# Three modulations' first column groups move from TensorE to VectorE, GLA's last gates move behind its results, and one set of norm factors goes

## The chip, the cores and the metric

The kernel runs as one program on one core of a Trainium2 chip. The metric is the device time of one execution in microseconds (us); the time of the kernel before is the median of three runs. All arithmetic is fp32. The engines are TensorE (PE, matmuls), VectorE (DVE), ScalarE (ACT), GpSimd (POOL) and SyncE (SP), whose queue issues nearly all DMAs.

## The reference

Two blocks of two layers each work on 256 tokens x and 256 context tokens, both of width 1024. Each layer has a modulation, a mixer (an attention with a hyena branch in the first block, DeltaNet and GLA in the second) and a feed-forward network (FFN):

```python
def modulation(cvec, w_mod, b_mod):
    m = (jax.nn.silu(cvec) @ w_mod + b_mod).reshape(-1, 1, N_MOD * D_MODEL)
    return jnp.split(m, N_MOD, axis=-1)          # 6 groups of 1024
def modulate(h, shift, scale):
    return h * (1.0 + scale) + shift
def squared_relu_ffn(h, w1, w2):                 # 1024 -> 4096 -> 1024
    return jnp.square(jax.nn.relu(h @ w1)) @ w2
...
sh1, sc1, g1, sh2, sc2, g2 = modulation(c, w_mod[l], b_mod[l])
csh1, csc1, cg1, csh2, csc2, cg2 = modulation(c_ctx, w_mod[l], b_mod[l])
hx = modulate(rms_norm(x, norm1_g[l]), sh1, sc1)
hc = modulate(rms_norm(xc, norm1_g[l]), csh1, csc1)
...
x = x + g1 * mixer(hx, hc)
x = x + g2 * squared_relu_ffn(modulate(rms_norm(x, norm2_g[l]), sh2, sc2), w1, w2)
```

In the second layer of each block the context's own result is not needed, so of the modulation by c_ctx only the first two groups (shift and scale ahead of the mixer) are used there; in the first layers all six are. GLA's readout is `rms_norm(o) * silu(z)` for each of 4 heads, with z a projection (the gates) of the input, and a product with w_out behind it. setup_inputs scales the gains and context by fixed factors; it changes no shape.

## The kernel before, in words

Activations lie with features on the partitions: 128 x (8 blocks x 512 tokens, x then context). The program runs: the first block's layer 0 (0 to 304 us), its FFN on both streams ("2_0", 304 to about 700), layer 1 (700 to 873), its FFN on x alone (873 to about 1050), DeltaNet (to about 1800), the FFN of that layer on both streams ("4", 1820 to 2160), GLA (2170 to 2372) and the last FFN (to the end).

Weights. `weight` (L306 to L317) loads 128 x 1024 fp32 into `wr`, casts it on ACT to a rounded part `wh` (L315), and VectorE subtracts for the rest `wl` (L316). A product is three matmuls per 128 rows, `wh·rh`, `wh·rl` and `wl·rh`, in this order, in mm3 (L324, L325, L326) and in lins (L358 to L360); so each weight's third matmul already needs its `wl`. One weight with 512 columns is 24 matmuls. Raw weights have three buffers, and `wh` and `wl` four in the FFNs.

FFN. `lins` works the first four weights (24 matmuls for each weight and stream). Then each weight of the first matrix gives one hidden block: ACT does the ReLU (L639), VectorE multiplies it into a square (h, L640), ACT and VectorE split it into two parts (r, L302 and L303). The second matrix (`tail`) adds its results to xs on VectorE (L689).

Modulation (L375 to L441). silu(c) for both c lies in `cvs`, 32 columns wide. By default each of the six groups of 1024 output columns is computed on PE: three rows of blocks (3 x 128 inputs) per step are loaded into `wm`, and multiplied in 32-column matmuls into `pmd` (L402); then ACT copies out, four small matmuls with a selection matrix (L413) turn the result, and VectorE adds the bias (L414). With `rows` given (a1, the first block's layer 1, and b1, the second block's layer 1), groups 2 to 5 come instead from rows: the transposed weight, 128 output features x 1024 inputs per row, is multiplied on VectorE with silu(c), copied on all partitions as `cb`, and summed in the same instruction (L437), for the one c that is needed, three rows per step. `cb` is loaded and put through Silu on ACT as an FFN begins (L588 to L591).

Order of the background. All modulations but the first are a list of pairs of load and computation, `bg`: a1, then b0, then b1. `load_ahead` issues loads, `background(n)` does n steps, `slot()` does one step per `every` slots, where the first matrix of an FFN gives a slot per hidden block and the second per output block; `quota` limits the number of steps that an FFN starts. FFN "2_0" has quota 35 and every 1.5, FFN "4" quota 17 and every 3. Each engine does its instructions strictly in its own program order, as the scheduler set it; a row on VectorE thus stands ahead of the `wl`, `h` and `r` behind it.

Norm factors. `stat_end` sums squares over the partitions with two matmuls (L472) and takes the reciprocal root in 13 small VectorE operations (rsqrt, L452 to L464). `first_layer` calls it twice over at its end (L1095 and L1096): the first set, `ys`, is read by nobody.

GLA (L1748 on). For each of four heads it calls values, the head's prepare, finish (masked products `pad`, results `ppo`, norm, written to `ot`), readout of the head before (transposes `pgt<-ot`, multiplication with the gate z, L1739, and a split) and gate (48 matmuls for z, and Silu) of the head after. In the order of before, gate(3) stands ahead of finish(3). The last readout is called from within the product with w_out.

## Time and profile before, and how to read it

| what | value |
|---|---|
| median of 3 runs | 2589.76 us (2586.95 to 2590.99) |
| the profiled execution | 2585.91 us |
| its span in the profile, mean granted clock of PE | 2584.1 us, 0.981 |
| busy: PE, VectorE, ScalarE, GpSimd | 95%, 67%, 44%, 9% |
| chain that ended last: PE, VectorE, issue | 77%, 10%, 5% |
| modulation matmuls into pmd (L402), rows on VectorE (L437) | 896, 64 |

A busy share says how much of the span an engine had an instruction under way, not that it waited for nobody. Which engine sets the end of a stretch is read from that stretch: from its windows (busy time and clock), and from the waits of the engine that is full there. The clock is given as a share of full speed: 1.00 is 2.4 GHz and 0.50 is 1.2 GHz. Line numbers are those of the kernel before.

### The profile page before, as it was taken

Reading aid. Unit: us, or ns where it says so; the run is one execution under the profiler, and the core shown is the slowest. Engines: PE = TensorE matmul, PEld = TensorE weight load, DVE = VectorE, ACT = ScalarE, POOL = GpSimd, SP = SyncE. Lnnn points to the kernel's source line nnn. Section 1 sums busy time; section 2 is a strip of 40 time slices with the busy share of each in tenths; the row PEclk is TensorE's granted clock in tenths of the full one; section 3 lists DMA queues with packets and bytes.
Section 4 is the critical chain, followed back from the end, with each engine's and each line's share of the span. In section 5 each row is a group of like instructions: output and inputs, shape, how many; then the busy total and the mean of one; then the engine's idle time right before and its main releaser. Section 6 shows DMA issues by size and latency. Waiting matters only on the chain.

```text
span 2584.1 us, 39685 instructions
## 1 busy us (share of the span) xinstructions
PE 2463.6 (95%) x15196; PEld 2082.7 (81%) x15196; DVE 1721.3 (67%) x3659; ACT 1133.8 (44%) x2157; POOL 235.2 (9%) x217
## 2 busy tenths in 40 slices
PE   7999999999999899998999999987999999899999
PEld 4766788777886899977778777876878888788999
DVE  5555558333567677898877877878458446777766
ACT  3345423222355455673545444544322334654544
POOL 0000000000000000111233323200000000220000
PEclk8999999999999999999999999999999999999999
DMA  7334468565241456322122212211567332222665
GB/s 273 110 133 150 155 216 323 199 228 174 83 134 63 140 178 206 122 66 56 31 66 66 56 42 68 67 44 50 180 215 256 98 98 82 77 82 72 188 182 156
DMA packets 147359, 335.08 MB, mean 130 GB/s; under 512 B 57134, under 2 KB 68512, under 8 KB 147168
## 3 DMA queue, kind: packets, MB, share of 16 engines
q1 hardware_dynamic: 146912, 332.46, 40.5%
q8 instruction: 120, 1.97, 0.3%
q14 instruction: 71, 0.58, 0.1%
q0 software_dynamic: 256, 0.07, 0.0%
HBM read 328.81 MB, written 3.67 MB: 129 GB/s over the span
## 4 chain that ended last, share of the span: by engine, by line
PE 77%; DVE 10%; issue 5%; ACT 3%; DMA 3%; POOL 1%; SPq 0%; DVEq 0%; ACTq 0%; POOLq 0%
PE pmm L324 19%; PE pmm L326 18%; PE pmm L325 18%; PE pmd L402 2%; DVE wl L316 1%; DMA wm<-wmod 1%; PE ps L1035 1%; ACT wh L315 1%; PE pmm L359 1%; PE pa L1395 1%; PE pa L1371 1%; PE pmm L358 1%; PE pmm L360 1%; PE pa L1413 1%; PE pa L1366 1%
## 5 line engine op out<-in xcount | busy, mean ns | idle before, releaser
L315 ACT CAST wh<-wr 128x1024 fp32r<-128x1024 f32 (+1 forms) x421 | 425.8, 1015 | 687.0 <-PE pmm L325 481.4
L324 PE MATMUL pmm<-h,wh 128*128 128x512 f32 (+2 forms) x1800 | 626.4, 348 | 8.0 <-ACT E L860 1.9
L316 DVE TENSOR_TENSOR wl<-wr,wh 128x1024 fp32r<-128x1024 f32 (+1 forms) x381 | 448.6, 1179 | 275.9 <-ACT wh L315 269.2
L326 PE MATMUL pmm<-h,wl 128*128 128x512 f32 (+2 forms) x1800 | 622.0, 346 | 9.7 <-DVE wl L316 9.7
L325 PE MATMUL pmm<-h,wh 128*128 128x512 f32 (+2 forms) x1800 | 619.1, 344 | 0.0
L326 PE MATMUL pmm<-r,wl 128*128 128x256 f32 (+1 forms) x1280 | 435.0, 341 | 2.6 <-DVE wl L316 2.5
L324 PE MATMUL pmm<-r,wh 128*128 128x256 f32 (+1 forms) x1280 | 435.4, 341 | 1.9 <-DVE q L1020 1.4
L325 PE MATMUL pmm<-r,wh 128*128 128x256 f32 (+1 forms) x1280 | 433.8, 339 | 0.0
L324 PEld LDWEIGHTS pmm<-h,wh 128*128 128x128 f32 x1800 | 342.2, 190 | 56.8 <-issue 6.7
L326 PEld LDWEIGHTS pmm<-h,wl 128*128 128x128 f32 x1800 | 342.5, 190 | 54.2 <-DVE wl L316 11.7
L325 PEld LDWEIGHTS pmm<-h,wh 128*128 128x128 f32 x1800 | 342.5, 190 | 39.5 <-issue 0.8
L324 PEld LDWEIGHTS pmm<-r,wh 128*128 128x128 f32 x1280 | 241.3, 189 | 33.8 <-issue 7.6
L326 PEld LDWEIGHTS pmm<-r,wl 128*128 128x128 f32 x1280 | 241.6, 189 | 28.9 <-DVE wl L316 4.7
L325 PEld LDWEIGHTS pmm<-r,wh 128*128 128x128 f32 x1280 | 241.8, 189 | 23.2 <-issue 1.7
L689 DVE SCALAR_TENSOR_TENSOR xs<-pmm,modb,xs 128x256 f32<-128x256 f32 x232 | 106.6, 478 | 101.6 <-PE pmm L326 101.5
L542 POOL TENSOR_TENSOR h<-n,h 128x256 fp32r<-128x256 f32 x28 | 21.4, 764 | 1218.9 <-ACT h L541 1218.5
L689 DVE SCALAR_TENSOR_TENSOR xs<-pmm,moda,xs 128x256 f32<-128x256 f32 x120 | 54.4, 480 | 110.8 <-PE pmm L326 110.6
L302 ACT CAST r<-h 128x256 fp32r<-128x256 f32 (+1 forms) x128 | 65.7, 514 | 123.6 <-DVE h L640 67.6
L316 POOL TENSOR_TENSOR wl<-wr,wh 128x1024 fp32r<-128x1024 f32 x40 | 96.2, 2406 | 146.8 <-ACT wh L315 112.9
L303 DVE TENSOR_TENSOR r<-h,r 128x256 fp32r<-128x256 f32 (+1 forms) x128 | 71.0, 556 | 32.7 <-ACT r L302 29.8
L437 DVE SCALAR_TENSOR_TENSOR wm<-wm,cb 128x1024 f32<-128x1024 f32 x64 | 76.4, 1220 | 4.2 <-DMA wm<-amodr 2.4
L1397 ACT COPY e<-pa 128x256 f32<-128x256 f32 x64 | 23.8, 372 | 122.5 <-PE pa L1395 121.8
(501 smaller groups left out, 3889.5 us busy)
## 6 DMA issues: line engine op xcount, KB each, us to landing
wr<-w SPq DMA_DIRECT2D x128, 512.0 KB
wr<-f SPq DMA_DIRECT2D x128, 512.0 KB
wr<-dwin SPq DMA_DIRECT2D x49, 512.0 KB
wm<-amod SPq DMA_DIRECT2D x16, 1536.0 KB
wm<-wmod SPq DMA_DIRECT2D x12, 1536.0 KB
wm<-wmodr SPq DMA_DIRECT2D x10, 1536.0 KB
wm<-amodr SPq DMA_DIRECT2D x10, 1536.0 KB
wr<-win SPq DMA_DIRECT2D x28, 512.0 KB
```

Source lines behind the costliest of these rows:

```text
L302: self.nc.scalar.copy(hi, src)
L303: self.nc.vector.tensor_tensor(lo, src, hi.bitcast(F32), ALU.subtract)
L315: self.nc.scalar.copy(hi, raw)
L316: (self.nc.gpsimd if self.pool_lo else self.nc.vector).tensor_tensor(lo, raw, hi.bitcast(F32), ALU.subtract)
L324: mm(ps, wh[:, k, :], rh[:, n0:n1], start=k == 0, stop=False)
L325: mm(ps, wh[:, k, :], rl[:, n0:n1], start=False, stop=False)
L326: self.mark = mm(ps, wl[:, k, :], rh[:, n0:n1], start=False, stop=k == last)
L358: mm(ps[:, c0:c1], wh[:, k, :], rh[:, c0:c1], start=k == 0, stop=False)
L359: mm(ps[:, c0:c1], wh[:, k, :], rl[:, c0:c1], start=False, stop=False)
L402: self.last = nc.tensor.matmul(ps[32 * c : 32 * c + 32, :256], cs[:, k + i, :], raw[:, i, 256 * c : 256 * c + 256], start=k + i == 0, stop ...
L437: nc.vector.scalar_tensor_tensor(raw[:, i], raw[:, i], 1.0, self.cb, ALU.mult, ALU.mult, accum_out=m[:, i : i + 1])
L689: self.nc.vector.scalar_tensor_tensor(x, ps, mod[:, 8 * gch + m, v : v + 1], x, ALU.mult, ALU.add)
```

## The change

1. a1, b0 and b1: groups 0 and 1 now come from rows on VectorE too, for both c: eight steps of two rows, each with four multiplications (two rows, both c), so 32 rows' multiplications for each modulation instead of two PE groups. a1 and b1 are now wholly on VectorE; of b0, groups 2 to 5 stay on PE, ahead of its rows. The first product of a row for the other c is written to a spare slot of the tile.
2. `cb` holds both c, 128 x 2048, in a new function `rows_c`; the second block's is loaded within FFN "2_0" at b0's first step, and again as FFN "4" begins.
3. FFN "2_0": quota 39 and every 1.4; FFN "4": 19 and 2.8.
4. GLA: gate(3) behind finish(3), and the readout of head 2 behind gate(3); `ot` has two buffers.
5. The unread set `ys` at the end of `first_layer` goes: of layer 0 for both streams, of layer 1 for x.

```diff
-        nc.gpsimd.memset(mod[:, 16:, 1], 0.0)
+
+        rows, one = rows
+        if one:
+            nc.gpsimd.memset(mod[:, 16:, 1], 0.0)
...
         def rstep(j, n, raw):
-            m = mod[:, 16 + j : 16 + j + n, 0]
             for i in range(n):
-                nc.vector.scalar_tensor_tensor(raw[:, i], raw[:, i], 1.0, self.cb, ALU.mult, ALU.mult, accum_out=m[:, i : i + 1])
-            nc.vector.tensor_tensor(m, m, self.small(bname)[:, 16 + j : 16 + j + n], ALU.add)
-
-        rs = [(lambda j=j, n=min(3, 32 - j): rload(j, n), lambda raw, j=j, n=min(3, 32 - j): rstep(j, n, raw)) for j in range(0, 32, 3)]
-        return mod, [s for cc in range(2) for s in steps(cc)] + rs
+
+                for v in (1, 0) if j < 16 else (0,):
+                    nc.vector.scalar_tensor_tensor(raw[:, i if v == 0 else self.wide - 1], raw[:, i], 1.0, self.cb[:, v], ALU.mult, ALU.mult,
+                                                   accum_out=mod[:, j + i, v : v + 1])
+            m = mod[:, j : j + n, :] if j < 16 else mod[:, j : j + n, 0:1]
+            nc.vector.tensor_tensor(m, m, self.small(bname)[:, j : j + n].unsqueeze(2).to_broadcast([P, n, m.shape[2]]), ALU.add)
+
+        js = [(j, 2) for j in range(0, 16, 2)] + ([(j, min(3, 48 - j)) for j in range(16, 48, 3)] if one else [])
+        rs = [(lambda j=j, n=n: rload(j, n), lambda raw, j=j, n=n: rstep(j, n, raw)) for j, n in js]
+        if one:
+            return mod, rs
+        rest = [s for cc in range(2, 6) for s in steps(cc)]
+
+        load, comp = rest[0]
+        rest[0] = load, lambda raw: (self.rows_c("cb2"), comp(raw))[1]
+        return mod, rest + rs
+
+    def rows_c(self, name):
+        self.cb = self.t("cb", 2048).rearrange("p (v n) -> p v n", v=2)
+        self.nc.sync.dma_start(self.cb, self.a[name])
+        self.nc.scalar.activation(self.cb, self.cb, AF.Silu)
...
-        ys = [self.stat_end(S, k) for k in "xc"[:NS]]
         return [self.stat_end(S, k) for k in "xc"] if both else (h, S)
...
-        for hd in range(4):
-            if hd < 3:
-                vn = values(hd + 1)
-                c1 = next(cg)
-            if ot is not None:
+        for hd in range(3):
+            vn = values(hd + 1)
+            c1 = next(cg)
+            if hd:
                 with self.tc.issue_after(self.mark.ins):
                     og += readout(hd - 1, ot, zo)
-            if hd < 3:
+
+            if hd < 2:
                 zn = gate(hd + 1)
-                nxt = prepare(hd + 1, *c1, vn)
+            nxt = prepare(hd + 1, *c1, vn)
             ot, zo = finish(hd, vt, *cur), zs
-            if hd < 3:
-                cur, vt, zs = nxt, vn, zn
+            cur, vt, zs = nxt, vn, zn
+        o3 = finish(3, vt, *cur)
+        zs = gate(3)
+        with self.tc.issue_after(self.mark.ins):
+            og += readout(2, ot, zo)
...
-                            mods2.extend(self.modulation(f"amod_{j}", f"abmod_{j}", "cv2", f"b{j}", rows="amodr_1" if j else None) for j in range(2))
+                            mods2.extend(self.modulation(f"amod_{j}", f"abmod_{j}", "cv2", f"b{j}", rows=(f"amodr_{j}", j == 1)) for j in range(2))
...
-                    self.ffn(xs, "g2_0", "w1_0", "w2_0", mods[0][0], "2_0", both, ys, None, 35, 1.5, S, None, before, lambda sv: f["then"](sv), cb="cb")
+                    self.ffn(xs, "g2_0", "w1_0", "w2_0", mods[0][0], "2_0", both, ys, None, 39, 1.4, S, None, before, lambda sv: f["then"](sv), cb="cb")
...
-        self.ffn(xs, "fg_0", "f1_0", "f2_0", mods2[0][0], "4", both, None, h, 17, 3, S, None, before, lambda sv: f["then"](sv), [both[1], both[0]], "cb2")
+        self.ffn(xs, "fg_0", "f1_0", "f2_0", mods2[0][0], "4", both, None, h, 19, 2.8, S, None, before, lambda sv: f["then"](sv), [both[1], both[0]], "cb2")
```

The order of instructions, first excerpt: VectorE in FFN "2_0", from the `wl` of the fifth weight on. Before:

```order
L316 TENSOR_TENSOR wl<-wr,wh 128x1024
L640 TENSOR_TENSOR h<-h,pmm 128x512 x3
L303 TENSOR_TENSOR r<-h,r 128x512
L316 TENSOR_TENSOR wl<-wr,wh 128x1024
L303 TENSOR_TENSOR r<-h,r 128x512
L640 TENSOR_TENSOR h<-h,pmm 128x512
L303 TENSOR_TENSOR r<-h,r 128x512
L316 TENSOR_TENSOR wl<-wr,wh 128x1024
```

After; the `wl` of the fifth weight and three h stand right above (the line numbers are those of the changed kernel, where L655 is h, L302 r, L440 a row and L315 wl):

```order
L302 TENSOR_TENSOR r<-h,r 128x512
L440 SCALAR_TENSOR_TENSOR wm,moda_118<-wm,cb 128x1024
L302 TENSOR_TENSOR r<-h,r 128x512
L655 TENSOR_TENSOR h<-h,pmm 128x512
L302 TENSOR_TENSOR r<-h,r 128x512
L440 SCALAR_TENSOR_TENSOR wm,moda_118<-wm,cb 128x1024
L302 TENSOR_TENSOR r<-h,r 128x512
L655 TENSOR_TENSOR h<-h,pmm 128x512
L440 SCALAR_TENSOR_TENSOR wm,moda_118<-wm,cb 128x1024
L302 TENSOR_TENSOR r<-h,r 128x512
L440 SCALAR_TENSOR_TENSOR wm,moda_118<-wm,cb 128x1024
L315 TENSOR_TENSOR wl<-wr,wh 128x1024
```

The `wl` of the sixth weight stood right behind the first r; now five h, five r (with those above) and four rows of a1 lie between the two `wl`.

Second excerpt: VectorE at the beginning of FFN "4", from the norm's last h. Before:

```order
L527 SCALAR_TENSOR_TENSOR e<-xs,gs_16766,pb 128x256
L538 SCALAR_TENSOR_TENSOR h<-e,modb_391,h 128x256 x2
L316 TENSOR_TENSOR wl<-wr,wh 128x1024
L640 TENSOR_TENSOR h<-h,pmm 128x512 x3
L303 TENSOR_TENSOR r<-h,r 128x512
L316 TENSOR_TENSOR wl<-wr,wh 128x1024
```

After:

```order
L555 SCALAR_TENSOR_TENSOR h<-e,modb_391,h 128x256 x2
L440 SCALAR_TENSOR_TENSOR wm,modb_392<-wm,cb 128x1024 x5
L315 TENSOR_TENSOR wl<-wr,wh 128x1024
L655 TENSOR_TENSOR h<-h,pmm 128x512 x3
L302 TENSOR_TENSOR r<-h,r 128x512
L443 TENSOR_TENSOR modb_392<-modb_392,abmod_17280 128x4
L315 TENSOR_TENSOR wl<-wr,wh 128x1024
```

Five rows of b1 now stand between the norm and the fifth weight's `wl`.

Third excerpt: PE at the end of GLA, from the results of head 3's second half (`ppo`); `pgt<-k_id,ot` are the transposes of a readout. Before:

```order
L1723 MATMUL ppo<-v,Ao 128x256
L1724 MATMUL ppo<-v,A 128x256
L326 MATMUL pmm<-h,wl 128x256
L324 MATMUL pmm<-h,wh 128x256
L325 MATMUL pmm<-h,wh 128x256
L326 MATMUL pmm<-h,wl 128x256
L324 MATMUL pmm<-h,wh 128x256
L325 MATMUL pmm<-h,wh 128x256
L326 MATMUL pmm<-h,wl 128x256
L478 MATMUL pgt<-k_id,ot 128x128 x4
L324 MATMUL pmm<-h,wh 128x256 x2
```

After:

```order
L1737 MATMUL ppo<-v,Ao 128x256
L1738 MATMUL ppo<-v,A 128x256
L325 MATMUL pmm<-h,wl 128x256
L323 MATMUL pmm<-h,wh 128x256
L324 MATMUL pmm<-h,wh 128x256
L325 MATMUL pmm<-h,wl 128x256
L323 MATMUL pmm<-h,wh 128x256
L324 MATMUL pmm<-h,wh 128x256
L325 MATMUL pmm<-h,wl 128x256
L495 MATMUL pgt<-k_id,ot 128x128 x4
L323 MATMUL pmm<-r,wh 128x256
L324 MATMUL pmm<-r,wh 128x256
```

Before, the transposes that end this piece are those of head 3's readout, and the next matmul needs what comes of them; the matmuls ahead are the first of the product with w_out. Now the matmuls around `ppo` are those of gate(3), the transposes are those of head 2's readout, and head 3's come 36 matmuls later.

## Rows read from the trace of the kernel before

**Rows 1.** The page, busy time: us, share of the span, instructions.

```profile
PE 2463.6 (95%) x15196; PEld 2082.7 (81%) x15196; DVE 1721.3 (67%) x3659; ACT 1133.8 (44%) x2157; POOL 235.2 (9%) x217
```

**Rows 2.** Windows: length, busy us of PE, PEld, DVE, ACT, POOL; clock, DMA share, GB/s.

```profile
400.00:410.00 10.00, 9.83 (x43) 7.81 (x42) 9.53 (x17) 2.78 (x3) 0.00 (x0) 1.00 0.96 388
365.00:700.00 335.00, 334.83 (x1801) 264.37 (x1800) 170.80 (x271) 94.43 (x129) 0.31 (x1) 1.00 0.61 214
...
878.00:884.00 6.00, 5.75 (x27) 5.66 (x28) 2.04 (x14) 0.00 (x0) 0.00 (x0) 0.51 0.32 109
2366.00:2379.00 13.00, 8.60 (x35) 7.45 (x36) 8.43 (x23) 4.20 (x8) 0.00 (x0) 0.61 0.17 48
```

**Rows 3.** All waits of PE from 365 to 700: total us, times, longest.

```profile
PE pmm L326 <- DVE wl L316: 0.2, 1, 0.2
```

**Rows 4.** Timeline of PE before the second layer's MLP: start, duration, instruction.

```profile
877.81 0.98 PE L472 MATMUL pt<-ones,xs 128*128 128x1 f32 x4 [4.14 <-DVE xs L503]
879.04 0.58 PE L324 MATMUL pmm<-h,wh 128*128 128x258 f32 x1 [0.25 <-DVE tm L474]
```

**Rows 5.** Timeline of PE at the end of GLA.

```profile
2365.47 0.28 PE L326 MATMUL pmm<-h,wl 128*128 128x256 f32 x1
2368.47 1.20 PE L478 MATMUL pgt<-k_id,ot 128*128 128x128 f32 x4 [2.72 <-DVE ot L1729]
2370.69 0.80 PE L324 MATMUL pmm<-h,wh 128*128 128x256 f32 x2 [1.01 <-ACT h L302]
```

**Rows 6.** Timeline of PE around a modulation step of 24 matmuls.

```profile
468.15 0.39 PE L325 MATMUL pmm<-r,wh 128*128 128x512 f32 x1
...
469.06 0.39 PE L326 MATMUL pmm<-r,wl 128*128 128x512 f32 x1
469.37 1.50 PE L402 MATMUL pmd<-wm,cvs 128*32 128x256 f32 x24
470.81 0.50 PE L324 MATMUL pmm<-r,wh 128*128 128x512 f32 x1
```

**Rows 7.** Timeline of PE around the end of a group.

```profile
347.15 0.39 PE L326 MATMUL pmm<-h,wl 128*128 128x512 f32 x1
...
347.74 0.49 PE L324 MATMUL pmm<-h,wh 128*128 128x512 f32 x1
```

**Rows 8.** Groups of VectorE's instructions, 365 to 700: busy, mean ns; idle before.

```profile
L316 DVE TENSOR_TENSOR wl<-wr,wh 128x1024 fp32r<-128x1024 f32 x57 | 69.7, 1223 | 52.5 <-ACT wh L315 52.3
L437 DVE SCALAR_TENSOR_TENSOR wm<-wm,cb 128x1024 f32<-128x1024 f32 x32 | 38.2, 1219 | 1.8 <-DMA wm<-wmodr 1.8
```

**Rows 9.** Timeline of VectorE among rows.

```profile
435.60 1.22 DVE L316 TENSOR_TENSOR wl<-wr,wh 128x1024 fp32r<-128x1024 f32 x1
436.74 1.22 DVE L437 SCALAR_TENSOR_TENSOR wm<-wm,cb 128x1024 f32<-128x1024 f32 x1
...
437.88 0.69 DVE L640 TENSOR_TENSOR h<-h,pmm 128x512 f32<-128x512 f32 x1
438.48 1.22 DVE L316 TENSOR_TENSOR wl<-wr,wh 128x1024 fp32r<-128x1024 f32 x1
```

**Rows 10.** Timeline of PE at the beginning of FFN "2_0".

```profile
309.36 1.19 PE L484 MATMUL pa<-k_id,rsy 128*128 128x128 f32 x4 [2.83 <-DVE rst L462]
...
312.75 2.79 PE L402 MATMUL pmd<-wm,cvs 128*32 128x256 f32 x24
315.47 0.58 PE L358 MATMUL pmm<-h,wh 128*128 128x256 f32 x1
...
339.29 0.28 PE L360 MATMUL pmm<-h,wl 128*128 128x256 f32 x1
...
376.09 0.49 PE L324 MATMUL pmm<-r,wh 128*128 128x512 f32 x1
```

**Rows 11.** Timeline of VectorE there, the fifth weight.

```profile
339.49 1.23 DVE L316 TENSOR_TENSOR wl<-wr,wh 128x1024 fp32r<-128x1024 f32 x1 [16.16 <-ACT wh L315]
```

**Rows 12.** Timeline of ACT at the beginning of FFN "4".

```profile
1830.93 1.06 ACT L591 ACTIVATE cb<-cb 128x1024 f32<-128x1024 f32 x1 [9.17 <-DMA cb<-cb]
```

More of the change, by code (lines that the diff above doesn't have):

```diff
@@ L40, in _rows @@
 def _rows(w):
-    return _c(w[:, 2048:].T.reshape(32, P, 1024))
+    return _c(w.T.reshape(-1, P, 1024))
 def _slabs(w):
@@ L141, in host_arrays @@
     a["cv2"] = _c(np.stack([i["c_2"][0], i["c_ctx_2"]], 0).reshape(2, 8, P).transpose(2, 1, 0))
-    for n, c in (("cb", "c"), ("cb2", "c_2")):
-        a[n] = _c(np.broadcast_to(i[c][0], (P, 1024)))
-    a["wmodr_1"], a["amodr_1"] = _rows(i["w_mod"][1]), _rows(i["ada_w_2"][1])
+    for n, c, cc in (("cb", "c", "c_ctx"), ("cb2", "c_2", "c_ctx_2")):
+        a[n] = _c(np.broadcast_to(np.stack([i[c][0], i[cc]], 0), (P, 2, 1024)))
+    a["wmod_0"], a["wmodr_1"] = _moving(i["w_mod"][0]), _rows(i["w_mod"][1])
+    a["amod_0"], a["amodr_0"], a["amodr_1"] = _moving(i["ada_w_2"][0]), _rows(i["ada_w_2"][0][:, :2048]), _rows(i["ada_w_2"][1])
     for l in range(2):
@@ L147, in host_arrays @@
         a[f"g2_{l}"] = _fm(i["norm2_g"][l])
-        a[f"wmod_{l}"] = _moving(i["w_mod"][l])
         a[f"bmod_{l}"] = _fm(i["b_mod"][l])
@@ L174, in host_arrays @@
         a[f"w2_{l}"] = _slabs(i["w_mlp2"][l])
-        a[f"amod_{l}"] = _moving(i["ada_w_2"][l])
         a[f"abmod_{l}"] = _fm(i["ada_b_2"][l])
@@ L581, in ffn @@
         with ExitStack() as st:
-            self.pools(st, dict(n=(8, 256), h=3, acc=(4, 256), sq=(4, 256), rs=(1, 258), cb=(1, 1024)), dict(a=2, md=1, mm=5), 12 if one else 18, "a", quota)
+            self.pools(st, dict(n=(8, 256), h=3, acc=(4, 256), sq=(4, 256), rs=(1, 258), cb=(1, 2048)), dict(a=2, md=1, mm=5), 12 if one else 18, "a", quota)
             self.wp2 = self.lo
@@ L588, in ffn @@
             if cb:
-                self.cb = self.t("cb", 1024)
-                self.nc.sync.dma_start(self.cb, self.a[cb])
-                self.nc.scalar.activation(self.cb, self.cb, AF.Silu)
+                self.rows_c(cb)
             self.background(1 if every < 2 else 0)
@@ L1801, in run @@
                         next(filt)
-                        mods = [self.modulation(f"wmod_{j}", f"bmod_{j}", "cv", f"a{j}", 3, 0 if j else 2, "wmodr_1" if j else None) for j in range(2)]
+                        mods = [self.modulation(f"wmod_{j}", f"bmod_{j}", "cv", f"a{j}", 3, 0 if j else 2, ("wmodr_1", True) if j else None) for j in range(2)]
                         self.bg = mods[0][1]
@@ L1931, in run @@
             h = 256
-            sb = dict(n=(6, h), low=1, k=4, q=(4, h), z=(4, h), kE=(2, h), kt=(2, h), S=(4, h), qe=(4, h), Ao=(1, h), part=2, A=(2, P), ot=1)
+            sb = dict(n=(6, h), low=1, k=4, q=(4, h), z=(4, h), kE=(2, h), kt=(2, h), S=(4, h), qe=(4, h), Ao=(1, h), part=2, A=(2, P), ot=2)
             self.pools(st, sb, dict(gt=2, ad=2, po=1, mm=3), 4, "gt")
```

2 lines of the change are left out of this document (1 added, 1 removed).

## The prediction

> **What bounds the kernel now.** I read the page first: PE is busy 95% of the span [rows 1]. So the question is stage by stage what PE does there and who makes it wait. The table of windows comes next [rows 2]: in the feed-forward stretch from 365 to 700 us PE is busy 334.83 of 335.00 us at full clock, and the list of waits has one wait of PE on a weight's low part there, 0.2 us [rows 3]. In that stretch a PE instruction removed is time removed, as long as VectorE keeps up. VectorE is the engine to watch: where rows of a modulation already run on it, it is busy 9.53 of 10 us [rows 2]. Two other places are not full: PE stands 4.14 us before the second layer's MLP and then runs at a clock of 0.51 [rows 2, 4], and at the end of GLA it stands 2.72 and 1.01 us and the clock falls to 0.61 [rows 2, 5].
>
> **Prices.** On PE, 24 modulation matmuls (3 rows of blocks) put 470.81 - 469.06 = 1.75 us between two matmuls that otherwise start 0.23 apart (468.15 to 469.06, four of them, 0.227 each): 1.52 us, and 1.62 with the slower first matmul behind them [rows 6]. A step of two blocks, scaled by 16/24 on the 1.5, is 1.1 to 1.2. The four selecting matmuls at a group's end cost 347.74 - 347.15 - 0.23 = 0.36, 0.46 with the slow start [rows 7]. A group is 2 x 1.62 + 1.18 + 0.46 = 4.88 us, two groups 9.76, and three modulations lose two groups each. On VectorE a row takes 1.219 us by duration [rows 8] and 1.14 from start to start; h and a weight's low part (wl) start 0.60 and 1.14 apart [rows 9], and I take 0.60 for r, the same shape. A new row step (two rows, both c) is 4 x 1.14 plus its bias, 4.65 us; 24 of them add 110 us of VectorE work, hidden only where PE has more to do than VectorE.
>
> **The change, part by part.**
>
> A, modulation a1, from 312 us. Before, 2.72 us of modulation matmuls run right before the first MLP matmul at 315.47 [rows 10]. They go, and of four chains of norm factors two go, 26 small VectorE operations; of the 2.83 us that PE waits for such factors at 309.36 I take 1.6. The MLP's first four weights then end at 315.47 - 2.7 - 1.6 + 23.9 (their length, 192 matmuls, [rows 10]) + 0.4 (more of them at half clock) = 335.5. Four more weights and the first of the second matrix, 24 matmuls x 0.227 = 5.45 us each, would let the tenth weight start at 335.5 + 5 x 5.45 = 362.7, against 376.09: 13.4 us gained. But VectorE's new order (first excerpt of the order) has 5 h, 5 r and 4 rows between the fifth and sixth wl: 5 x 0.60 + 5 x 0.60 + 4 x 1.14 + 1.14 = 11.7 us. The fifth wl ends at about 337.3 (before, it was done 1.2 us after the last matmul of the first four weights [rows 10, 11], and its cast stays bound to them; now one row is ahead of it by then), the sixth at 349.0. PE has finished weight five at 336.7 + 5.45 = 342.1 and can begin weight six three matmuls ahead of its wl's end: it stands 6.3 us. Carried on in the same way, it stands 1.2 at weight five and 2.0 at weight eight. A = 13.4 - 9.4 = **4.0**. Bounds: 13.4, if nothing waits as [rows 3] has it; -2, if the clock falls after two of these stalls, as it did for about 6 us after the 4.14 us stall, each costing 3 [rows 2, 4]. I take 4.0, nearest to the counted order. The Trainium skill ("TensorE: Matmul & The Clock Gate", HAM oscillation) says that waits between stretches of matmuls bring the slow clock back for the next stretch; the trace agrees where PE stood 4.14 us, and by that rule A would be about 1.
>
> B, modulation b0, same MLP from about 450 us: 9.76 of PE goes. From here a row step falls on 1.4 slots. With 1.4 weights of the first matrix VectorE needs 4.65 + 1.4 x (1.14 + 0.60 + 0.60) = 7.9 us against PE's 1.4 x 5.45 = 7.6; with those of the second it needs less, since no h and r are formed there. It is even, on 3 to 4 weights of lead; I count one stall of 0.6. B = **9.2**. Bounds 5 (each of 8 steps late by 0.3, and twice that) to 9.8. The second load of c's rows is 1 MB and one Silu on ACT, ahead of weight casts that have three weights of lead: nothing. DMA: a step brings 1.0 MB of rows and 0.7 MB of weights in 7.6 us, 223 GB/s, where rows of before had up to 388 [rows 2].
>
> C, modulation b1, next MLP from 1837 us: again 9.76. Five rows now stand ahead of the fifth wl (second excerpt of the order). The Silu of c's rows began at 1830.93, once their DMA had come [rows 12]; with twice the elements it ends near 1833, and 5 x 1.14 + 1.14 behind it make 1840. PE could begin the fifth weight at about 1837 and waits 2.5 us; counted on in the same way, it waits 0.9 at the seventh. With a row step on 2.8 slots VectorE is otherwise idle enough (4.65 + 2.8 x 2.34 = 11.2 of 15.3 us). C = **6.4**, bounds 3 (both stalls doubled) to 9.8.
>
> D, one set of norm factors fewer in the second layer. PE waits 4.14 us for the sum that only this dead set needs next, spends 0.98 on it, waits 0.25 more, and begins at half clock [rows 4]. In the new order the first 258-column matmul stands right behind the tail and waits only for its own tiles. Its last tile is written when that sum is (about 878), so the first weight ends near 878.6 rather than 884. D = **5**, bounds 1.5 (the 0.98 + 0.25, and little else) to 6 (the stall and the whole slow clock).
>
> E, GLA's last gates behind its results. PE's last 48 gate matmuls (5.8 us at the 0.12 of [rows 10]) move from ahead of head 3's results to where PE waits for their masks and norm (third excerpt of the order). The readout of head 3, at 2368.47 [rows 5], should come about as much earlier, and PE's two waits (3.73) and the 13 us at a clock of 0.61 (5 us lost) [rows 2] shrink. E = **7**, bounds 0 (the same wait elsewhere) to 10 (waits and slow clock gone). Below zero is excluded but for the Silu's table load that moves with the gates, 1.3 us.
>
> The moved preparation of cv2, the memsets and the table load lie on ACT and POOL beside other work: nothing. More buffers (ot, cb) cost no time.
>
> **Sum.** 4.0 + 9.2 + 6.4 + 5 + 7 = 31.6. The profiled execution took 2585.91, so 2554.3. The median of the runs is 3.85 above it: **2558**. All lower bounds together would be a gain of 6 (-2 + 5 + 3 + 1.5 - 1.3), all upper ones 49.
>
> **The instruction's own price.** A row multiplies two fp32 operands in SBUF and takes 1.219 us for 1024 elements, the same as wl's plain subtraction, 1.223 [rows 8]. The Trainium skill ("Vector Engine (DVE) Microarchitecture Reference", Points that are easy to get wrong) says that scalar_tensor_tensor with two non-bf16 sources in SBUF runs at half throughput; by that a row would have to be 2.4 us, a new step 9.5 against PE's 7.6, and A and B losses. The row is of this very instruction, so it decides.
>
> **Rivals.**
>
> (1) VectorE becomes the bound in the 16 new steps of the first MLP (7.9 against 7.6 us, and 9.53 of 10 us busy already [rows 2]). Then A and B vanish and C, D, E stay: gain 18.4, 2571. For: the closeness. Against: at 9.5 tenths PE waited 0.2 us in 335 [rows 3]. Chance 0.12.
>
> (2) The norm and GLA gains turn into other waits (PE waits for the last h at 878 anyway; head 3's readout waits for the moved gates' Silu). D + E = 2: gain 21.6, 2568. Chance 0.12.
>
> (3) Slower: wl is late behind every 4-row step, the lead being used up and never rebuilt. Between two wl then lie 4.65 + 1.20 + 1.14 = 7.0 us against 5.45: 1.5 us for each of 24 steps, 37 in all, and half the time at half clock behind eight of them (3 us each [rows 2, 4]), 24 more: 61 lost of 31.6 gained, 2619. It decides once stalls in the row stretches exceed 31.6 / 24 = 1.3 us a step. Against: in before's 11 steps of 3 rows this didn't happen [rows 3]. Chance 0.05.
>
> (4) The change does not do what it says. The new order shows the modulation matmuls gone, so I leave it nothing.
>
> **How the numbers follow.** The forecast has 0.71, rivals 1 to 3 have 0.12, 0.12 and 0.05. 0.2% of the time is 5.2 us, about what a measurement of this kernel can tell from no change. A gain under 5.2 needs rival 1 with C, D or E failing too: I give 0.05 out of rival 1 and the lower bounds. So faster 0.89, same 0.05, slower 0.06 (rival 3 and 0.01 of still worse clocks). The range goes from 2547 (a gain of 43, most upper bounds at once) to 2577 (a gain of 13: D and E, or rival 1 with C at its lower bound); above lie rival 3 and the near ties, below the last upper bounds.
>
> **What would show it.** Right, if in the profile after: modulation matmuls fall from 896 to 512 and rows rise from 64 to 160 at the same 1.22 us; the first MLP shows PE waiting on wl near 342 to 349 us for about 6 us, and less than 2 us afterwards; the second layer's MLP starts without a 4 us gap; and the clock near GLA's end stays near 1. Wrong, if PE's waits on wl between 335 and 700 sum to more than 20 us (rivals 1, 3), if rows take over 2 us, or if the gaps of [rows 4, 5] come back under other names.

## The result, and the profile after

The changed kernel takes **2558.02 us** (median of 4 runs, 2556.43 to 2558.93); the kernel before, run with it again, 2588.36. The ratio is 0.9883 with a 95% interval of [0.9866, 0.9900], some 30 us faster. The profiled execution took 2558.93 us (span 2557.2). Against the profile of before it is 27.0 us shorter, a little less than the medians are apart.

The page's busy line, and the group of the rows (the same columns as in [rows 1] and [rows 8]):

```profile
PE 2433.3 (95%) x14776; PEld 2067.1 (81%) x14776; DVE 1826.2 (71%) x3830; ACT 1135.7 (44%) x2152; POOL 238.9 (9%) x217
...
L440 DVE SCALAR_TENSOR_TENSOR wm<-wm,cb 128x1024 f32<-128x1024 f32 x160 | 192.8, 1227 | 27.6 <-DMA wm<-amodr 12.6
```

Beside [rows 1]: PE is busy 30 us less, VectorE 105 us more. The modulation matmuls went from 896 to 512 and the rows from 64 to 160. A row takes 1.227 us in the mean, against 1.219 in [rows 8]; the last section says why. PE is still the engine with the largest busy share.

Windows of the changed kernel (length; busy PE, PEld, VectorE, ACT, POOL; clock, DMA share, GB/s), beside [rows 2]:

```profile
344.00:348.00 4.00, 0.32 (x2) 0.00 (x0) 4.00 (x8) 0.62 (x1) 0.00 (x0) 0.81 0.00 0
348.00:352.00 4.00, 2.62 (x6) 2.14 (x7) 4.00 (x8) 0.00 (x0) 0.00 (x0) 0.50 0.59 196
365.00:700.00 335.00, 332.12 (x1717) 267.60 (x1715) 223.79 (x388) 100.22 (x139) 2.95 (x4) 1.00 0.63 222
2340.00:2350.00 10.00, 7.16 (x49) 5.86 (x48) 7.77 (x20) 4.23 (x10) 0.00 (x0) 1.00 0.17 52
```

In the long feed-forward stretch PE is idle 2.9 us of 335. 1.3 us of that lie behind 697, where the next layer begins already, and four waits for a weight's low part sum to the other 1.6. Ahead of it, from 344 to 352, there is a hole that was not there before, and a clock of 0.50 behind it. All waits of PE on a low part from 304 to 700 us (total, times, longest), where the kernel before had the 0.2 of [rows 3]:

```profile
PE pmm L325 <- DVE wl L315: 7.2, 6, 5.1
```

The longest of them, on PE's timeline (start, duration; idle before and its releaser):

```profile
310.92 1.01 PE L357 MATMUL pmm<-h,wh 128*128 128x256 f32 x3
...
337.65 0.50 PE L325 MATMUL pmm<-h,wl 128*128 128x512 f32 x1 [0.53 <-DVE wl L315]
...
343.93 0.39 PE L324 MATMUL pmm<-h,wh 128*128 128x512 f32 x1
349.38 0.80 PE L325 MATMUL pmm<-h,wl 128*128 128x512 f32 x1 [5.06 <-DVE wl L315]
...
353.36 0.40 PE L325 MATMUL pmm<-h,wl 128*128 128x512 f32 x1
```

and VectorE's order at the same place, from the fifth weight's low part (`wl`) to the sixth's:

```profile
336.38 1.23 DVE L315 TENSOR_TENSOR wl<-wr,wh 128x1024 fp32r<-128x1024 f32 x1 [1.12 <-DMA wm<-wmodr]
337.52 1.88 DVE L655 TENSOR_TENSOR h<-h,pmm 128x512 f32<-128x512 f32 x3
...
339.91 1.22 DVE L440 SCALAR_TENSOR_TENSOR wm<-wm,cb 128x1024 f32<-128x1024 f32 x1
...
346.95 1.22 DVE L440 SCALAR_TENSOR_TENSOR wm<-wm,cb 128x1024 f32<-128x1024 f32 x1
...
348.10 1.22 DVE L315 TENSOR_TENSOR wl<-wr,wh 128x1024 fp32r<-128x1024 f32 x1
```

The fifth `wl` ends at 337.6 and the sixth at 349.3; the prediction had 337.3 and 349.0. Between them stand the h, r and rows of the first excerpt, without a gap. PE had done six matmuls of the sixth weight's first two products by 344.3 and then stood 5.06 us. The nine matmuls from 349.38 to 353.36 then took 4.0 us, where nine at full clock take 2.0 (0.227 from start to start).

Where the 27 us lie, from the same instruction in both timelines (us from the span's start). The gain of a stretch is the difference between the two lengths:

| from this instruction to the next | before | after | gained |
|---|---|---|---|
| a weight cast late in layer 0 | 293.2 | 294.5 | -1.3 |
| first result added in FFN "2_0" (tenth weight begins) | 375.93 | 372.90 | +4.3 |
| last result added in FFN "2_0" | 708.99 | 697.05 | +8.9 |
| first 258-column matmul of layer 1's MLP | 879.04 | 863.81 | +3.3 |
| first result added in that MLP | 915.38 | 904.34 | -4.2 |
| first ReLU of FFN "4" | 1837.20 | 1825.29 | +0.9 |
| first subtraction for GLA's masks (VectorE, `LV<-cum`) | 2229.81 | 2210.78 | +7.1 |
| first 258-column matmul of the last FFN | 2397.31 | 2369.57 | +8.7 |
| last result added | 2580.61 | 2553.55 | -0.7 |

The first line is time that the changed kernel's profile lost ahead of any changed work. The others are, in this order, terms A (4.3), B (8.9), D (3.3 - 4.2 = -0.9), 0.9 without a term, C (7.1), E (8.7) and -0.7 behind it. This is one profile of each kernel. How far one profile can be off shows in E's stretch: it took 163.2 to 167.5 us in the four kernels of this document that have the old order of GLA, and 158.4 to 160.7 in the ten that have the new one. That is 5.3 us in the mean, and the 8.7 of this pair stands at the upper end.

**Where term D went.** PE, layer 1's MLP, beside [rows 4]:

```profile
863.81 0.39 PE L323 MATMUL pmm<-h,wh 128*128 128x258 f32 x1 [1.54 <-DVE xs L704]
...
867.04 0.50 PE L489 MATMUL pa<-ones,xs 128*128 128x1 f32 x4
...
884.88 0.58 PE L323 MATMUL pmm<-h,wh 128*128 128x258 f32 x1 [5.27 <-DVE h L650]
```

The first 258-column matmul waits 1.54 us in place of 4.14 and 0.25, and the slow clock that [rows 2] had there is gone: the start is as forecast. But 16 us later PE stands 5.27 us for h, the product with the norm factors, and the slow clock comes behind this stall instead:

```profile
885.00:889.00 4.00, 4.00 (x19) 4.00 (x20) 2.82 (x6) 2.02 (x4) 0.00 (x0) 0.50 0.60 152
```

In the kernel before, the two longest waits of PE from 860 to 920 us were these:

```profile
PE pt L472 <- DVE xs L503: 4.1, 1, 4.1
PE pmm L324 <- DVE h L635: 1.1, 1, 1.1
```

ScalarE of the changed kernel shows what was ahead of that h:

```profile
877.67 0.42 ACT L518 ACTIVATE acc<-xs 128x256 f32<-128x256 f32 x1 [6.12 <-DMA xs<-ctx]
...
878.61 1.03 ACT L314 CAST wh<-wr 128x1024 fp32r<-128x1024 f32 x1
...
882.53 0.36 ACT L508 COPY rs<-pa 128x256 f32<-128x256 f32 x1
884.87 0.51 ACT L651 ACTIVATE h<-h 128x256 f32<-128x256 f32 x1 [1.97 <-DVE h L650]
```

`rs`, the copy of the norm factors, is queued behind weight casts and behind the first squares of the *context*, which is being loaded anew for the second block. The first square waits 6.12 us for that DMA. And the DMA could not start earlier, because x's sum of squares lies in the context's place of xs until the matmul at 867.04 has read it:

```profile
867.57 0.60 SPq L1882 DMA_DIRECT2D xs<-ctx  x1
```

So the norm that comes earlier makes PE wait for the norm factors, which stand behind the reload in ScalarE's order. The issue comes 17.1 us earlier than before (884.71), the square only 13.0 (890.63 before): from issue to square it is now 10.1 us, against 5.9. Why the transfer takes longer was not looked into.

**The end of GLA**, beside [rows 5]:

```profile
2344.07 0.60 PE L495 MATMUL pgt<-k_id,ot 128*128 128x128 f32 x4
...
2345.68 0.50 PE L323 MATMUL pmm<-h,wh 128*128 128x256 f32 x2 [1.01 <-ACT h L301]
```

The wait of 2.72 us for `ot` is gone, the 1.01 us for h has stayed. The clock is 1.00 there.

### The profile page after: what moved, and what is told of

Read it like the earlier page. It is cut to its first block, busy times and chain, and to the rows that moved or that the text cites. A ratio compares the mean times of both kernels' runs of the same rounds, so it can differ in the third digit from the quotient of the medians.

```text
span 2557.2 us, 39019 instructions
## 1 busy us (share of the span) xinstructions
PE 2433.3 (95%) x14776; PEld 2067.1 (81%) x14776; DVE 1826.2 (71%) x3830; ACT 1135.7 (44%) x2152; POOL 238.9 (9%) x217
## 3 DMA queue, kind: packets, MB, share of 16 engines
q1 hardware_dynamic: 147152, 334.56, 40.5%
## 5 line engine op out<-in xcount | busy, mean ns | idle before, releaser
L315 DVE TENSOR_TENSOR wl<-wr,wh 128x1024 fp32r<-128x1024 f32 (+1 forms) x381 | 448.7, 1180 | 212.9 <-ACT wh L314 205.1
L440 DVE SCALAR_TENSOR_TENSOR wm<-wm,cb 128x1024 f32<-128x1024 f32 x160 | 192.8, 1227 | 27.6 <-DMA wm<-amodr 12.6
L559 POOL TENSOR_TENSOR h<-n,h 128x256 fp32r<-128x256 f32 x28 | 24.3, 871 | 991.6 <-ACT h L558 939.1
L315 POOL TENSOR_TENSOR wl<-wr,wh 128x1024 fp32r<-128x1024 f32 x40 | 96.1, 2403 | 146.7 <-ACT wh L314 112.9
L302 DVE TENSOR_TENSOR r<-h,r 128x256 fp32r<-128x256 f32 (+1 forms) x128 | 71.0, 556 | 25.5 <-ACT r L301 22.3
```

Of the source, the lines that this page charges most:

```text
L302: self.nc.vector.tensor_tensor(lo, src, hi.bitcast(F32), ALU.subtract)
L315: (self.nc.gpsimd if self.pool_lo else self.nc.vector).tensor_tensor(lo, raw, hi.bitcast(F32), ALU.subtract)
L440: nc.vector.scalar_tensor_tensor(raw[:, i if v == 0 else self.wide - 1], raw[:, i], 1.0, self.cb[:, v], ALU.mult, ALU.mult, accum_out=mod[ ...
L559: (nc.gpsimd if pool and j in (0,2,4,6) else nc.vector).tensor_tensor(lo, t, hi.bitcast(F32), ALU.subtract)
```

## The experiments

All times are medians, and ratios are against the kernel before run on the same chip with them. That one had medians of 2586.67 to 2588.36 us beside them, and the changed kernel itself was timed in the first set alone. A ratio is good to 2 to 5 us, the half width of its interval, and a difference between two rows is no better; smaller ones rest on the waits in the profiles.

| run | us | ratio, 95% interval |
|---|---|---|
| changed kernel | 2558.02 | 0.9883 [0.9866, 0.9900] |
| norm factors alone | 2586.19 | 0.9988 [0.9979, 0.9997] |
| GLA's order alone | 2581.65 | 0.9978 [0.9970, 0.9986] |
| modulations alone | 2569.47 | 0.9929 [0.9918, 0.9941] |
| changed, context's squares late | 2555.04 | 0.9871 [0.9857, 0.9886] |
| before, context's squares late | 2585.77 | 0.9995 [0.9986, 1.0004] |
| changed, rows four slots later | 2556.99 | 0.9880 [0.9864, 0.9897] |
| changed, both of these | 2554.49 | 0.9867 [0.9848, 0.9886] |
| changed, one row more per step | 2575.25 | 0.9954 [0.9942, 0.9967] |
| changed, without GpSimd in the norm | 2565.98 | 0.9924 [0.9908, 0.9940] |
| changed, rows and PE steps in turn | 2549.72 | 0.9853 [0.9835, 0.9870] |
| the same, one row more per step | 2557.09 | 0.9886 [0.9869, 0.9902] |
| in turn, context's squares late | **2543.54** | 0.9834 [0.9818, 0.9850] |

### The parts, each alone

**Norm factors alone**: the kernel before with one line less.

```diff
-        ys = [self.stat_end(S, k) for k in "xc"[:NS]]
```

> The kernel before with the unread norm factors taken out and nothing else. Theory (from the two traces): the matmul that opens the second layer's MLP comes some 5 us earlier, but the gain is given back within 30 us, because ScalarE's queue has the first square of the reloaded context ahead of weight casts and of the copy of the norm factors, and that square waits for a DMA of 1 MB which can only start when the norm's sum has been read. So 1 to 3 us faster in all, nearly all of it from the first layer: about 2586, with a wait of PE for h (the product with the norm factors) that grows from 1.1 to about 5 us. Rival (the prediction's term): 5 us from the second layer and 1.6 from the first, about 2582, and that wait stays near 1.

Measured 2586.19, 1.7 us under the 2587.89 of its own runs of before, 3.1 by the ratio of 0.9988. The longest wait of PE in layer 1's MLP:

```profile
PE pmm L324 <- DVE h L635: 4.2, 1, 4.2
```

The 4.1 us for the sum are gone, and the 1.1 us for h have become 4.2. The rival, which was the prediction's term D, is out: what PE gains at the start of this MLP it loses some 16 us later. From the MLP's first matmul to its first result this run takes 39.8 us (876.69 to 916.44), against 36.3 in the kernel before and 40.5 in the changed one.

**GLA's order alone**: the loop over heads and the second `ot` buffer as in the change, on the kernel before.

> The kernel before with GLA's new order and two ot buffers, nothing else. Theory: 6 to 8 us faster, about 2581; the wait of 2.7 us for ot at the end of GLA is gone or under 1, and the clock between GLA's last results and the last FFN stays above 0.9. Rival: the Silu of the last gates becomes the new last thing that the readout waits for, and the gain is under 3 us.

Measured 2581.65, 6.2 us faster. All waits of PE from 2330 to 2385 us of that run:

```profile
PE pmm L326 <- DVE wl L316: 1.2, 2, 0.8
PE pmm L324 <- ACT h L302: 1.0, 1, 1.0
PE pmm L324 <- ACT wh L315: 0.6, 1, 0.6
```

No wait for `ot` is left, and the clock is 1.00 from 2366 to 2379, where [rows 2] has 0.61. The last gates' Silu cost nothing that shows. Alone the order gave 6.2 by the medians, and 5.3 in the mean over all profiles; the 8.7 above is from one pair of them.

**Modulations alone**: the changed kernel with GLA's loop and the line of `ys` as before.

> The changed kernel with GLA's order of before and with the unread norm factors kept: only the three modulations' first groups on VectorE, with the new quotas. Theory: the parts add up, so 30 less about 8 (GLA) and less about 1 to 2 (first layer's norm factors) remain, 19 to 21 us faster than before: about 2568. Of it 10 to 12 come by the end of the first MLP, 7 in the MLP after DeltaNet. Rival: with the norm factors kept, VectorE is too late for its first three row steps and the stall at the fifth to sixth weight grows: under 15 us faster, above 2573.

Measured 2569.47, 18.4 faster than its runs of before. In its profile 10.9 us of this are gained by the end of the first MLP, as expected, and 5.0 in FFN "4", where 7 were. The three parts sum to 18.4 + 6.2 + 1.7 = 26.3; together they gave 30.3. The ratios' parts, 0.0071 + 0.0022 + 0.0012 = 0.0105 against 0.0117, differ by less than the interval's half width, so they add as far as this can tell.

### Term D: who holds the norm factors

**Context's squares late**, on the changed kernel:

```diff
-                            for k in range(8):
-                                self.stat(S, "c", xs[:, k, 256:])
+                            with self.tc.issue_after(self.relu.ins):
+                                for k in range(8):
+                                    self.stat(S, "c", xs[:, k, 256:])
```

where `self.relu` is the last ReLU on ScalarE, here that of the MLP's second slab (a quarter of its hidden blocks); the line that sets it is left out.

> The changed kernel, with the eight squares of the reloaded context put on ScalarE behind the second slab's last ReLU of the second layer's MLP. Theory: PE's wait of 5.3 us for h in that MLP falls under 1, and 4 to 6 us are gained on the changed kernel: about 2553. Rival: something else holds the norm factors there (their own chain on VectorE, the weights' DMA): the wait stays above 3 and the time within 1.5 us of the changed kernel.

Measured 2555.04, 3.0 us under the changed kernel; the two ratios' intervals overlap, so the waits have to show it. The two longest of PE in that MLP (850 to 910 us), and the only one behind them (890 to 965 us):

```profile
PE pmm L323 <- ACT wh L314: 1.2, 1, 1.2
PE pmm L323 <- DVE h L650: 1.2, 1, 1.2
```

```profile
PE pa L489 <- DVE acc L520: 1.2, 1, 1.2
```

The wait for h fell from 5.3 to 1.2, the clock stays at 1.00 there, and another 1.2 us came up, for a weight cast: with the squares away, ScalarE's next cast waits for its own weight's DMA, 3.69 us, and the norm factors still stand behind it. The runs further on say the same of h: 5.0 and 3.5 us with the squares early (rows four slots later; rows and PE steps in turn), 0.5 and 1.2 with the squares late in addition to these. That the squares of the context held the factors is shown; that they alone did so is not so. The gain is less than the 4 to 6 expected because part of it is given back: PE now waits 1.2 us for the context's sum itself, and from the first slab's last result to the second's first it takes 31.9 us, against 30.0 in the changed kernel. The other three runs with late squares have the same 31.9 to 32.0.

**The same edit on the kernel before.**

> The kernel before with the context's squares late on ScalarE. Theory: there PE's wait for h at that place is only 1.1 us, since the unread norm factors keep PE late anyway, so this gives 0 to 1.5 us: about 2587. With the 3 us that the same edit gives in the changed kernel, the norm factors' removal and the squares' place are one matter. Rival: the edit gives its 3 us here too, and has nothing to do with the norm factors.

Measured 2585.77, ratio 0.9995 with an interval that includes 1: nothing that can be told from no change. There PE comes to this place late in any case. The interval reaches to a gain of 3.6 us and so does not exclude the rival by itself; the profiles do. From the MLP's first matmul to its first result the late squares leave 33.8 us of 36.3 in the kernel before, and 33.1 of 40.5 in the changed one: 2.6 and 7.4 us gained, of which some 2 are given back behind it in both. So the removal of the norm factors and the place of the squares are one matter. Alone they give 1.7 us and, by the ratio, 1.3, the latter within what is no change; on top of the first, the second gives 3.0.

### Terms A and B: what VectorE can bear

**One row more per step**: in each of the 24 new row steps one multiplication is done twice.

```diff
-                for v in (1, 0) if j < 16 else (0,):
+                for v in ((1, 1, 0) if i == 0 else (1, 0)) if j < 16 else (0,):
```

> The changed kernel with one row multiplication more in each of the 24 new row steps (the first row's product with the other c is taken twice; the result is the same): 24 x 1.14 us, 27 us of VectorE work. Theory (VectorE and PE are nearly even in the first MLP's new row steps, and VectorE has room in the MLP after DeltaNet): of the 16 in the first MLP about half becomes a wait of PE for a low part: 4 to 10 us slower than the changed kernel, 2562 to 2568, with no change in the later MLP. If PE alone set the time: under 2 us. If VectorE set it: 18 us, 2576.

Measured 2575.25, 17.2 slower than the changed kernel: close to what was written down for "VectorE sets the time". The three longest waits from its first MLP:

```profile
PE pmm L325 <- DVE wl L315: 12.0, 5, 4.1
PE pmm L323 <- ACT wh L314: 5.8, 2, 5.0
PE pmm L323 <- DVE h L655: 2.1, 1, 2.1
```

The last result of FFN "2_0" is added at 711.97 in place of 697.05, 14.9 us later, for 16 x 1.14 = 18.3 us of work added there; FFN "4" adds about 1. My theory, that half of it would be hidden, was wrong. Of every microsecond that VectorE got to do in that MLP, PE paid some 0.8.

The 5.8 us for weight casts show a second path from VectorE to PE. SyncE's queue and ScalarE ahead of the wait of 5.0 us, which ends at 426.66:

```profile
409.51 6.07 SPq L433 DMA_DIRECT2D wm<-wmodr  x2
415.63 0.95 SPq L307 DMA_DIRECT2D wr<-w  x2
```

```profile
425.56 1.04 ACT L314 CAST wh<-wr 128x1024 fp32r<-128x1024 f32 x1 [1.86 <-DMA wr<-w]
```

The second of the two row loads (`wmodr`) is issued at 415.2, when VectorE's row of 413.96 has ended (415.18) and left its buffer free, and the weight loads behind it in the queue wait with it. A late VectorE thus makes weights late too, and not only their low parts.

**Rows four slots later**: three row steps as FFN "2_0" begins, and the next ones from four slots on.

```diff
-            self.background(1 if every < 2 else 0)
+            self.background(3 if every < 2 else 0)
...
-            self.every, self.slots, self.taken = every, 0, 0
+            self.every, self.slots, self.taken = every, -4 if every < 2 else 0, 0
```

> The changed kernel, where the first MLP does three row steps as it begins and then counts four slots fewer, so that the next row steps come behind the sixth weight's low part. Theory: the 5.1 us that PE stands at the sixth weight, and the slow clock behind it, are the price of four rows in that place and nothing else; the wait there falls under 1, at most 2 us come back at the eighth weight, and the kernel is 4 to 6 us faster than the changed one: about 2553. Rival: VectorE has no room in this stretch at all, the wait only moves, and the time stays within 1.5 us of the changed kernel's.

Measured 2556.99: the rival's outcome, though its four runs spread from 2550.53 to 2561.35, so that the time alone leaves room for the theory. Two of PE's waits from 300 to 700 us, and the window behind the first of them:

```profile
PE pmm L323 <- DVE h L655: 1.8, 1, 1.8
PE pmm L325 <- DVE wl L315: 1.7, 3, 0.8
```

```profile
340.00:344.00 4.00, 3.44 (x7) 1.85 (x8) 4.00 (x7) 3.02 (x5) 0.00 (x0) 0.52 0.64 241
```

The wait of 5.1 us on the low part is gone, but PE now waits 1.8 for h, and the clock falls at 340 instead of at 348. The rows that were pulled ahead stand in front of the norm's last h and of the first weights' h. The wait moved, and with it the slow clock; by the tenth weight the profile has gained 1.6 us.

**Both edits** (squares late, rows later).

> The changed kernel with both: the context's squares late on ScalarE (measured alone: 3 us) and the row steps of the first MLP four slots later. Theory: they lie in different stretches and add: 7 to 9 us faster than the changed kernel, about 2550. Rival: one of them is lost: 2553 to 2556.

Measured 2554.49, the same as the squares alone; the rival again.

**Rows and PE steps in turn.** VectorE is nearly full up to 450 us and then idle more than half of the time. These are windows of the changed kernel:

```profile
380.00:450.00 70.00, 68.38 (x298) 55.30 (x297) 65.05 (x116) 19.60 (x24) 0.00 (x0) 1.00 0.87 321
450.00:560.00 110.00, 110.00 (x629) 84.08 (x631) 42.23 (x60) 33.01 (x42) 0.00 (x0) 1.00 0.66 241
```

From 474 to 574 us b0's groups 2 to 5 are done on PE, and VectorE has 42 us of work in 110. This run does a1's 19 row steps and b0's 12 PE steps alternately; `cb` is reloaded at the last PE step (these lines are left out).

```diff
-                            self.bg = self.bg + mods[1][1] + mods2[0][1] + mods2[1][1]
+                            r, p = mods[1][1], mods2[0][1][:-8]
+                            mix = sorted([(i / len(r), 0, s) for i, s in enumerate(r)] + [((i + 2) / (len(p) + 1), 1, s) for i, s in enumerate(p)], key=lambda e: e[:2])
+                            self.bg = self.bg + [s for _, _, s in mix] + mods2[0][1][-8:] + mods2[1][1]
```

> The changed kernel with the steps of a1 (19, all rows) and those of b0 on PE (12) in turn, in place of a1's first; b0's own rows come last as before, and its load of c's rows moves to the last PE step. Theory (VectorE is full from 318 to about 450 us and idle more than half from 450 to 560, and only that full stretch makes PE wait): PE's waits on a low part from 300 to 700 us fall from 7.2 to under 3, the slow clock at 350 goes, and 4 to 8 us are gained: 2550 to 2554. Rival (as in the run with later rows): VectorE's backlog comes from the norm's operations and the first three steps before 340 us, and shows as a wait for h or r in place of the low part: within 2 us of the changed kernel.

Measured 2549.72, 8.3 us under the changed kernel (7.8 by the ratios). The profiled execution, 2543.99, is the fastest of its four. Its waits on a low part from 300 to 700, and the windows:

```profile
PE pmm L325 <- DVE wl L315: 0.5, 1, 0.5
```

```profile
340.00:380.00 40.00, 40.00 (x210) 31.12 (x209) 36.69 (x59) 14.56 (x19) 0.00 (x0) 1.00 0.76 273
380.00:450.00 70.00, 70.00 (x366) 55.07 (x366) 47.35 (x80) 20.01 (x26) 0.00 (x0) 1.00 0.74 268
450.00:560.00 110.00, 110.00 (x567) 87.21 (x567) 68.98 (x114) 31.94 (x41) 0.00 (x0) 1.00 0.73 269
```

The hole and the slow clock at 344 to 352 are gone (PE 40.00 of 40.00 at 1.00), and VectorE's work is spread: 47 of 70 and 69 of 110 us, where it was 65 and 42. The profile of the last run below, with the same order, has the same single wait of 0.5 us on a low part and a clock of 1.00 there. That the reload of `cb` moved as well was not tried by itself; where it lay in the changed kernel, PE was busy 110.00 of 110.00 us.

**The same with one row more per step.**

> The run with a1's rows and b0's PE steps in turn, with one row multiplication more in each of the 24 new row steps, as was done to the changed kernel, where it cost 17 us. Theory (VectorE set the time in the changed kernel's first MLP only because the row steps stood next to each other; spread, it has room): 0 to 5 us slower than the run in turn, 2550 to 2555. Rival (VectorE sets the time in that MLP whatever the order): 15 us or more, above 2564.

Measured 2557.09, 7.4 slower than without: between the two expectations. What the first MLP loses it loses before the tenth weight: the first result of FFN "2_0" is added at 375.13 in place of 367.73 (7.4 us), the last at 693.08 in place of 686.05 (7.0). Seven of the 16 added rows stand ahead of the first result in VectorE's order, some among the norm's operations; the nine others cost nothing there. These two profiles are 12.1 us apart, more than the medians, since that of the run in turn is its fastest; 2.4 of it lie between FFN "4"'s first ReLU and GLA, where the other eight added rows are. So VectorE's room depends on the order, and the first 60 us of that MLP had none for more even in the better order.

**In turn, and the context's squares late.**

> The same with the context's squares late on ScalarE. Theory: the gains add: 7 to 11 us under the changed kernel, 2547 to 2551, the fastest so far. Rival: only the squares' 3 us: 2555.

Measured 2543.54, ratio 0.9834: the fastest of all, 14.5 us under the changed kernel and 44 under the kernel before, more than was expected and than the two gains of 8.3 and 3.0 together. By the ratios it is 12.7 us against 7.8 and 3.1. The intervals of the ratios are 0.003 wide, 8 us, so that no more than the sum can be claimed.

## Why the prediction was right

The time was 2558 forecast and 2558.02 measured, inside the range of 2547 to 2577. By its own steps:

- **A, 4.0 forecast, 4.3 found, by misses that cancel.** The count of VectorE's new order gave the two `wl` within 0.3 us. The stall was 5.06 us rather than 6.3: PE came to the sixth weight 0.7 us later than counted and did six matmuls, not three, ahead of its `wl`. The waits of 1.2 and 2.0 us at the fifth and eighth weights came to 0.53 and next to nothing. The slow clock behind the stall came as well, 0.50 from 348 to 352, and cost some 2 us by the nine matmuls above; the sum had left it to the lower bound, at 3. What the Trainium skill says of waits and the slow clock ("TensorE: Matmul & The Clock Gate", HAM oscillation) agrees with this row. The first MLP matmul came 5.8 us earlier than before (310.92 less the 1.3 of the table's first line, against 315.47), where 4.3 were counted, and the first four weights took 25.5 us rather than 24.3.
- **B, 9.2 forecast, 8.9 found.** The sum was right. The reason I gave was only half so: I called VectorE and PE even and trusted the lead; the run with one row more showed that PE pays for some 0.8 of the VectorE work added to that MLP, and the run in turn showed 8 us that A and B leave there. The gain was that of the work taken from PE, less waits that come from the order of the steps (1.6 us in this stretch, where 0.6 was counted).
- **C, 6.4 forecast, 7.1 found (5.0 in the run of the modulations alone).** The wait was 1.1 us at the fifth weight in place of 2.5: the Silu of c's rows began 7.1 us ahead of the first ReLU, where it was 6.3 in the kernel before.
- **D, 5 forecast, -0.9 found: the step that failed.** "In the new order the first 258-column matmul stands right behind the tail" was right, and so were the 5 us that it gains: from the last matmul of the tail to the end of the first weight it was 10.95 us before (873.39 to 884.34) and is 5.22 now (861.98 to 867.20). But the working stopped at that weight. It did not ask what ScalarE has ahead of the copy of the norm factors, and that a reload of the context, bound to the same sum, is in that queue. PE stood 5.27 us for the factors, where it had stood 1.1, with the slow clock behind it. Of the prediction's own signs of being wrong one came about: the gap of [rows 4] came back under another name. Rival 2 had named such an exchange of one wait for another, with the last h and not with this DMA as its place; of its two halves this one happened, GLA's did not.
- **E, 7 forecast, 8.7 found in the one pair of profiles, 6.2 in the run of this part alone.** The last readout's transposes came 5.4 us earlier within GLA (2368.47 to 2344.07, less the 19.0 already gained), against 5.8 counted. Behind them the clock was 1.00 where [rows 2] had 0.61; that the rest is the clock's was not separated from the spread of single profiles.
- **Rival 1** (VectorE as the bound) was nearer than its 0.12: one more row per step gave 2575.25, beyond the rival's 2571. **Rival 3** did not come about: the waits on `wl` from 304 to 700 us sum to 7.2 us, not to 31.6. The rule on scalar_tensor_tensor that the prediction took from the Trainium skill ("Vector Engine (DVE) Microarchitecture Reference", Points that are easy to get wrong) and set aside would have shown in rows of 2.4 us, by the prediction's estimate; they took 1.23.

That the total agrees so closely is partly luck. D was 6 us too high, and the misses within A cancelled; C and E (0.7 and 1.7 above the forecast, in this pair of profiles) and the medians' distance from the profiles (30.3 against 27.0) made up for D.

## What to carry to other kernels

Follow a step that comes earlier on to the next place where it must wait, on every queue that it passes: here a square that waited for a DMA on ScalarE gave back all that one set of norm factors less had gained in that MLP. When work moves from a full engine to a second one, what counts is that engine's room in each stretch and not over the span; the same steps, alternated with steps that leave it free, gave 8 us more than in one block. Count the new order of the engine that takes the work between two things that the full engine needs; that gave the place of the new stall, and its length within 1.3 us, before anything ran.

## What the runs showed of the hardware that was not expected

Rows were slower while GpSimd worked. VectorE and GpSimd of the changed kernel, at the beginning of FFN "2_0":

```profile
316.08 1.23 DVE L440 SCALAR_TENSOR_TENSOR wm<-wm,cb 128x1024 f32<-128x1024 f32 x1 [0.34 <-ACT cb L458]
...
318.11 1.76 DVE L440 SCALAR_TENSOR_TENSOR wm<-wm,cb 128x1024 f32<-128x1024 f32 x1
...
319.80 1.75 DVE L440 SCALAR_TENSOR_TENSOR wm<-wm,cb 128x1024 f32<-128x1024 f32 x1
...
327.91 1.21 DVE L440 SCALAR_TENSOR_TENSOR wm<-wm,cb 128x1024 f32<-128x1024 f32 x1
```

```profile
313.33 0.74 POOL L559 TENSOR_TENSOR h<-n,h 128x256 fp32r<-128x256 f32 x1 [0.46 <-ACT h L558]
316.42 5.72 POOL L559 TENSOR_TENSOR h<-n,h 128x256 fp32r<-128x256 f32 x4 [2.35 <-ACT h L558]
```

Two rows that start while GpSimd does four subtractions take 1.76 and 1.75 us in place of 1.21, a third that starts in their last 0.3 us takes 1.35, and GpSimd's four take 1.43 us each in place of 0.74. The row at 316.08, under way when the four begin at 316.42, takes 1.23. With these subtractions on VectorE instead:

> The changed kernel with the four subtractions per stream of the first MLP's norm that GpSimd does given to VectorE. In the changed kernel, row multiplications that start at 318.1 and 319.8 us, while GpSimd is at these subtractions, take 1.76 and 1.75 us against 1.21 elsewhere, and GpSimd's four take 5.7 us where others take 0.75 each. Theory: the two engines keep each other from SBUF; with GpSimd idle every row there takes 1.21 to 1.24. Rival: the rows are slow because their data has just been written by a DMA or by ScalarE: 1.75 stays. For the time: VectorE loses 4 to 8 x 0.4 us by the added work and gains about 1.3 at the rows: within 2 us of the changed kernel.

The rows of that run (shortest, median and longest in ns):

```profile
L440 DVE SCALAR_TENSOR_TENSOR wm<-wm,cb x160: 1214/1219/1228, 317.5 to 1966.7; 128x1024 f32<-128x1024 f32 x160
```

None is above 1.228 us: the rival is out, and it was GpSimd's subtractions that slowed them. The Trainium skill ("SBUF — State Buffer", SBUF: two separate sides) says that VectorE and GpSimd share a pair of ports that only one may hold, an instruction of VectorE with two sources in SBUF among those that need it. The rows agree in that both engines get slower, and in that the row that was first did not. The time of that run was not as expected: 2565.98, 8 us slower than the changed kernel and not within 2. The eight subtractions are about 0.4 us each for VectorE, and the rows gained 1.2 us. How that came to 8 us is not shown. In the run's profile, 2562.25 and the fastest of its six, the first MLP is only 0.6 us behind at the tenth weight; it loses 4.8 more up to its last result, 3.0 of it in one wait of PE for a weight cast at 420.40, with a clock of 0.66 in the 10 us from there.
